# Leaving out the products with a zero state, and padding a triangular tile to 65 columns

## The chip, the cores and the metric

The kernel runs on one core of a Trainium2 chip. A core has five engines with a queue each: TensorE (PE, matrix products), VectorE (DVE), ScalarE (ACT), GpSimd (POOL), and SyncE (SP), which here only issues DMAs. The metric is the device time of one execution in microseconds (us); lower is better. The median of three runs of the kernel before is 2276.57 us (2274.77 to 2276.88).

## The reference

A trunk of two layers over 1024 positions and 1024 channels. A layer normalizes `x`, modulates it by a condition vector, projects it to 8320 columns, runs three causal mixers side by side, gates and merges them, and projects back. Two of the mixers carry a state through the sequence.

```python
# retention, 4 heads of 128, in chunks of C = 128 positions
def step(R, kv_n):
    return chunk_decay * R + kv_n, R
_, R_prev = lax.scan(step, jnp.zeros((B, H, dh, dh)), jnp.moveaxis(kv, 2, 0))
o = o_intra + einsum('bhnid,bhnde->bhnie', q_dec, R_prev)

# RWKV-7, 8 heads of 64, position by position
def step(S, inp):
    r_t, w_t, k_t, v_t, a_t, b_t = inp
    sa = einsum('bhvk,bhk->bhv', S, a_t)
    S = S * w_t[:, :, None, :] + sa[..., None] * b_t[:, :, None, :] + v_t[..., None] * k_t[:, :, None, :]
    return S, einsum('bhvk,bhk->bhv', S, r_t)
_, y = lax.scan(step, jnp.zeros((B, H, N, N)), xs)
```

Both states start at zero, and neither is returned.

## The kernel before

**Large products.** Almost all of PE's time goes to projections. Operands are split into a high and a low part of a faster 32-bit type, and each product is done as three: high by high, high by low, low by high, with 128x128 weights and 512 columns each. These are the groups `acc<-hhi,wh` and their like. Weights come by DMA as `wr`, ACT rounds them into `wh`, and POOL subtracts to get `wl`; `wh` and `wl` have three buffers each. A part of the projection is done late with combined matrices (Strassen's scheme), seen as `acc<-T,wh`.

**Small products.** The mixers use plain 32-bit products (F32), each of which PE does in two passes, so it stands in the trace as two records. A transpose on PE is one record.

**Retention** (`ret_task`): one task per head and layer, eight in all. A task works on two halves `h` of 512 positions, four chunks each: scores `rs`, transposed keys `rkt` (scaled as ACT takes them out), transposed values `rvt`, the chunk products `rkv`, then DVE chains the states `R`, and `ro` adds up the result. The eighth chunk's state is made, but no later chunk reads it.

**RWKV** (`rwkv_task`): one task per pair of heads and layer, eight in all, with 16 chunks of 64 positions each. `prepare` makes the decayed operands `AR` and `BK`; `scores` transposes `BK` into `BKt` (tile `bt`) and makes the triangular matrices `G`: 32 blocks of 128 columns, block `16*hd + c` for head `hd` and chunk `c`. `invert` and `blocks` invert the triangles in place; `states` multiplies `G` by the values into `AV` (tile `av`). After that the 16 chunks are stepped through, each as:

- ACT: `SP` is the state `S` times the chunk's decay `pc`.
- PE: `cy = AR^T S` (`two<-S,AR`), in one half of a PSUM tile `two`.
- DVE: `xst` is `cy` rows 64 to 127 plus `AV`.
- PE: `ch = G^T xst`, one product per head (`ch<-xst,G`); ACT copies it into `Z`.
- PE: `BKt^T Z` into `ch` (`ch<-Z,BKt`); DVE: the new state `S` from it and `SP`, one instruction per head.
- PE: `G^T Z` added to `cy` (`two<-Z,G`); ACT copies that to the output `y`.

In `av` and `ch` the weights are `G`'s columns from 64 of a block on, 65 of them, so that one column belongs to the next block and its result row is not used. The last block has no next one, and there 64 columns are taken (`n = min(65, ...)`).

**Order.** The generators only describe work. `Log.plan` takes all instructions with their dependences and modelled durations and builds one order for every engine: at each point the engine that is free first takes the ready instruction with the smallest key, and RWKV's work has a head start in it (`BIAS`). Every engine then runs its own list in that order. A tile comes from a pool with a fixed number of buffers, and the first instruction that touches a tile waits until a buffer is free. `G` has one buffer, which the RWKV tasks take in turn and which other stages of the layer use too (`gtile`).

Of the kernel before, what the change touches and what calls it, by code (L numbers as in the profile page):

```python
# [9 lines left out]
F32 = mybir.dt.float32  # L10
# [3 lines left out]
ALU = mybir.AluOpType  # L14
# [3 lines left out]
P = 128  # L18
# [538 lines left out]
def trunk_kernel(ctx, tc, xT, cvec, pos, vecs, consts, w_ada, w_all, pool_w, lora_w, out):  # L557
    nc = Log(tc.nc, tc)

    def pool(name, bufs, **kw):  # L560
        return PoolProxy(nc, ctx.enter_context(tc.tile_pool(name=name, bufs=bufs, **kw)), bufs, "")
# [1 line left out]
    cp = pool("cp", 1)  # L563
    hp_ = pool("hb", 32)
    wp = pool("wp", 2)
    gp = pool("gp", 1)
    rp = pool("rp", 4)
    tp = pool("tp", 4)
    mp = pool("mp", 4)
    sb = pool("sb", 1)  # L570
    sp = pool("sp", 2)
# [5 lines left out]
    uid = [0]  # L577

    def gtile(s):
        return gp.tile([P, 32 * P], F32, tag="G", name=nm(s))  # L580

    pin = lambda o: o

    def nm(s):
        uid[0] += 1
        return f"{s}_{uid[0]}"
# [624 lines left out]
    def ret_task(l, hd, qT, kT, vT, sg):  # L1211
        gC = math.exp(math.log1p(-(2.0 ** (-5.0 - hd))) * 128)
        dm = cs("causal", P).unsqueeze(1).to_broadcast([P, 4, P])
        hc = lambda k: cst[:, CST[k] + hd : CST[k] + hd + 1]
        tl, rg, eps_rh = hc("tail"), hc("rowg"), hc("reps")
        v3 = lambda t: t.rearrange("p (c n) -> p c n", n=P)
        prev = None
        for h in range(2):
            cl = lambda t, c: t[:, c * P : (c + 1) * P]
            yield wait(kT[h], qT[h])  # L1220
            ps = mx("rs")
            with nc.together():
                for c in range(4):
                    mmul(cl(ps, c), lhsT=cl(kT[h], c), rhs=cl(qT[h], c), start=True, stop=True)
            sm = mo("rsm")
            nc.vector.scalar_tensor_tensor(v3(sm), v3(ps), rg, dm, op0=ALU.mult, op1=ALU.mult)
            yield 1300
            yield wait(kT[h])
            ps = mx("rkt")
            with nc.together():  # L1230
                for c in range(4):
                    trans(cl(ps, c), cl(kT[h], c))
            kt = mo("rkt")
            nc.scalar.activation(kt, ps, AF.Copy, scale=tl)
            yield 900
            yield wait(vT[h])
            ps = mx("rvt")
            with nc.together():
                for c in range(4):
                    trans(cl(ps, c), cl(vT[h], c))  # L1240
            vt = mo("rvt")
            nc.scalar.copy(vt, ps)
            yield 600
            yield wait(kt, vt, spare=1000)
            kv = mx("rkv")
            with nc.together():
                for c in range(4):
                    mmul(cl(kv, c), lhsT=cl(kt, c), rhs=cl(vt, c), start=True, stop=True)
            R = []
            for c in range(4):  # L1250
                R.append(prev)
                nx = sb.tile([P, P], F32, tag="R", name=nm("R"), bufs=4)
                if prev is None:
                    nc.vector.tensor_copy(nx, cl(kv, c))
                else:
                    nc.vector.scalar_tensor_tensor(nx, prev, gC, cl(kv, c), op0=ALU.mult, op1=ALU.add)
                prev = nx
            yield 600
# [29 lines left out]
    def rwkv_task(l, hp, kT, rT, vp, lt, lw):  # L1288
# [1 line left out]
        AR = r8("AR").rearrange("p (c j t) -> p c j t", j=2, t=CH)  # L1290
        BK = r8("BK").rearrange("p (c j t) -> p c j t", j=2, t=CH)
        Gf = gtile("G")
        G = Gf.rearrange("p (u n) -> p u n", n=P)
        qa = lambda b: slice(64 + 32 * b, 96 + 32 * b)
        BKt = r8("BKt").rearrange("p (c n) -> p c n", n=P)
        Z = r8("Z").rearrange("p (c n) -> p c n", n=P)
# [96 lines left out]
        def scores(h):  # L1393
            yield max(until(whole[h] + 1000), wait(Z, spare=600))
            for q in range(2):
                ps = mx("bt")
                c0 = 8 * h + 4 * q
                with nc.together():
                    for c in range(4):
                        trans(ps[:, c * P : (c + 1) * P], jt(BK, slice(0, P), c0 + c), timed=True)  # L1400
                nc.scalar.copy(BKt[:, c0 : c0 + 4, :], ps.rearrange("p (c n) -> p c n", n=P))
                yield 1300
            for q in range(2):
                c0 = 8 * h + 4 * q
                gps = [mx("g"), cyt()]
                with nc.together():
                    for j in range(4):
                        for hd in range(2):
                            rows = slice(64 * hd, 64 * hd + 64)
                            mmul(gps[hd][:, j * P : (j + 1) * P], jt(BK, rows, c0 + j), jt(AR, rows, c0 + j), timed=True)  # L1410
                for hd in range(2):
                    u0 = 16 * hd + c0
                    nc.vector.tensor_tensor(
                        G[:, u0 : u0 + 4, :], gps[hd].rearrange("p (u n) -> p u n", n=P), rm, op=ALU.mult
                    )
                yield 2600
            yield from bonus(h)
# [46 lines left out]
        def states():  # L1464
            for q in range(4):
                yield wait(G, Z)
                ps = mx("av")
                with nc.together():
                    for j in range(8):
                        c, hd = 4 * q + j // 2, j % 2  # L1470
                        u0 = (16 * hd + c) * P + 64
                        n = min(65, 32 * P - u0)
                        mmul(ps[0:n, j * 64 : j * 64 + 64], Gf[:, u0 : u0 + n], Z[:, c, 64 * hd : 64 * hd + 64])
                nc.scalar.copy(AV[:, q * HF : (q + 1) * HF], ps[0:64, :])
                yield 1500
# [41 lines left out]
        for c in range(16):  # L1517
# [2 lines left out]
            if c % 8 == 0:  # L1520
                y = t_ri("y")
            S, Sn = SS[par], SS[1 - par]
            pcc = pc[:, c : c + 1]
            SP = sb.tile([P, P], F32, tag="SP", name=nm("SP"), bufs=1)
            nc.scalar.activation(SP, S, AF.Copy, scale=pcc)
            cy = cyt()
            sa = mmul(cy[:, 0:P], jt(AR, slice(0, P), c), S)
            if c:
                sa.no_dep = yout[-1]
                sa.after[yout[-1]] = 2  # L1530
            if c > 1:
                sa.own_dep = yout[-2]
            nc.vector.tensor_tensor(xst[0:64, :], cy[64:128, 0:P], AV[:, c * P : (c + 1) * P], op=ALU.add)
            yield wait(xst)
            ch = ps_c.tile([P, HF], F32, tag="ch", name=nm("ch"))
            for hd in range(2):
                cols = slice(64 * hd, 64 * hd + 64)
                u0 = (16 * hd + c) * P
                n = min(65, 32 * P - u0 - 64)
                mmul(ch[0:n, cols], Gf[:, u0 + 64 : u0 + 64 + n], xst[:, cols])  # L1540
            nc.scalar.copy(Z[0:64, c, :], ch[0:64, 0:P])
            yield wait(Z)
            mmul(ch[:, P : 2 * P], BKt[:, c, :], Z[:, c, :])
            for hd in range(2):
                rw = slice(64 * hd, 64 * hd + 64)
                nc.vector.scalar_tensor_tensor(
                    Sn[rw, rw], ch[rw, P + 64 * hd : P + 64 * hd + 64], pc[rw, c : c + 1], SP[rw, rw],
                    op0=ALU.mult, op1=ALU.add,
                )
# [854 lines left out]
```

## Time and profile before

| | |
|---|---|
| median of three runs | 2276.57 us (2274.77 to 2276.88) |
| span of the profiled execution | 2272.5 us; no other time is given for that execution, and the median stands 4.07 us above its span |
| PE busy | 2243.5 us, 99% |
| DVE, ACT, POOL busy | 71%, 41%, 28% |
| granted PE clock over the span | 0.996 |

How to read the profile's rows: a row of a group names the engine, the operation, the tile written and the tiles read, the shape, the number of records, busy time and the mean duration of one. Products overlap in PE's pipeline, so the mean of one (390 to 402 ns for a large product) is longer than the step from one start to the next. What a product costs PE is read from the timeline, whose rows begin with start and duration in us: the start of the next row minus the start of this one. Rows with "x4" merge neighbouring records of one kind. Idle time stands in brackets with what ended it.

### The profile page before, as it was taken

To read this page: it belongs to the slowest core of one execution; us is meant where nothing else is said; L and a number is where in the kernel's file an instruction comes from. 1 tells how busy PE (TensorE), PEld (TensorE's weight loads), DVE (VectorE), ACT (ScalarE), POOL (GpSimd) and SP (SyncE) were. 2 spreads that over 40 slices of the span, in tenths; PEclk is the share of its full clock that TensorE was granted. 3 is DMA by queue.
4 is the path that set the end of the run, shared out by engine and by line. 5 is a ranking of instruction groups with operands and counts; after the bars stand their busy time and mean duration, and the time that the engine had idled before them with its cause. 6 is when DMAs were issued, how large, how long until landed. Compare 5 with 4: busy or idle time off the path is not lost.

```text
span 2272.5 us, 35073 instructions
## 1 busy us (share of the span) xinstructions
PE 2243.5 (99%) x13076; PEld 1865.8 (82%) x13076; DVE 1612.3 (71%) x2776; ACT 934.5 (41%) x1795; POOL 629.1 (28%) x552
## 2 busy tenths in 40 slices
PE   7999999999999999999999999999999999999998
PEld 6788888888888888888888888888888888888888
DVE  7997786867878765677677678687785744465854
ACT  5644434434244334323454444344433444441243
POOL 2223323322326221331232232333431500041211
PEclk9999999999999999999999999999999999999999
DMA  9212111112236563654531111111112533256442
GB/s 323 70 56 68 33 47 39 52 43 62 89 112 228 195 216 112 228 191 165 174 129 38 38 38 35 56 43 48 53 62 84 190 117 112 88 181 217 134 130 84
DMA packets 138042, 248.85 MB, mean 110 GB/s; under 512 B 15632, under 2 KB 18960, under 8 KB 137872
## 3 DMA queue, kind: packets, MB, share of 16 engines
q1 hardware_dynamic: 137872, 246.61, 33.2%
q8 instruction: 103, 1.69, 0.3%
q14 instruction: 67, 0.55, 0.1%
HBM read 187.04 MB, written 59.51 MB: 108 GB/s over the span
## 4 chain that ended last, share of the span: by engine, by line
PE 90%; DVE 7%; ACT 1%; issue 1%; DMA 0%; POOL 0%; DVEq 0%; ACTq 0%; POOLq 0%
PE acc L543 74%; PE two L543 3%; PE ch L543 2%; PE g L543 1%; PE av L543 1%; PE ro L543 1%; DVE ksq L543 1%; PE m L543 1%; PE bt L543 1%; PE lw L543 1%; PE rkv L543 1%; PE rs L543 1%; DVE ada_ps L543 0%; DVE G L543 0%; PE pps L543 0%
## 5 line engine op out<-in xcount | busy, mean ns | idle before, releaser
L543 PE MATMUL acc<-hhi,wh 128*128 128x512 f32 x1488 | 597.9, 402 | 0.0
L543 PE MATMUL acc<-hhi,wl 128*128 128x512 f32 x1488 | 596.9, 401 | 0.0
L543 PE MATMUL acc<-hlo,wh 128*128 128x512 f32 x1488 | 596.2, 401 | 0.0
L543 POOL TENSOR_TENSOR wl<-wr,wh 128x512 fp32r<-128x512 f32 x167 | 225.4, 1351 | 568.0 <-ACT wh L543 421.8
L543 PEld LDWEIGHTS acc<-hhi,wh 128*128 128x128 f32 x1488 | 280.6, 189 | 49.8 <-issue 1.8
L543 PEld LDWEIGHTS acc<-hlo,wh 128*128 128x128 f32 x1488 | 280.5, 189 | 49.3 <-issue 1.1
L543 PEld LDWEIGHTS acc<-hhi,wl 128*128 128x128 f32 x1488 | 280.4, 188 | 49.4 <-issue 0.7
L543 ACT CAST wh<-wr 128x512 fp32r<-128x512 f32 x242 | 149.3, 617 | 265.7 <-PE acc L543 204.7
L543 PE MATMUL acc<-T,wh 128*128 128x512 f32 x576 | 178.2, 390 | 0.0
L543 DVE SCALAR_TENSOR_TENSOR S<-ch,pc,SP 64x64 f32<-64x64 f32 x256 | 72.2, 282 | 87.1 <-PE ch L543 84.0
L543 PEld LDWEIGHTS acc<-T,wh 128*128 128x128 f32 x576 | 108.0, 188 | 22.4
L543 PE MATMUL acc<-T,wl 128*128 128x512 f32 x288 | 112.4, 390 | 0.0
L543 DVE TENSOR_TENSOR wl<-wsum,wh 128x512 fp32r<-128x512 f32 x69 | 49.2, 712 | 81.8 <-ACT wh L543 81.5
L543 ACT CAST wh<-wsum 128x512 fp32r<-128x512 f32 x96 | 59.5, 620 | 95.0 <-PE acc L543 92.9
L543 POOL TENSOR_TENSOR oz<-ol,oz 128x512 fp32r<-128x512 f32 x10 | 14.0, 1401 | 281.7 <-DVE wl L543 212.6
L543 DVE TENSOR_TENSOR xst<-two,MT 64x128 f32<-64x128 f32 x128 | 37.6, 293 | 68.4 <-PE two L543 47.7
L543 DVE TENSOR_TENSOR two<-two,tm 64x30 f32<-64x30 f32 (+14 forms) x240 | 78.9, 329 | 7.3
L543 ACT COPY Z<-ch 64x128 f32<-64x128 f32 x128 | 33.0, 258 | 123.3 <-PE ch L543 123.2
L543 DVE TENSOR_TENSOR tm<-MT,two 64x30 f32<-64x30 f32 (+14 forms) x240 | 76.3, 318 | 10.2 <-ACT two L543 3.4
L543 PE MATMUL acc<-oy,wh 128*128 128x512 f32 x256 | 80.1, 394 | 0.0
L543 PE MATMUL acc<-oz,wh 128*128 128x512 f32 x256 | 79.0, 389 | 0.0
L543 PE MATMUL acc<-oG,wh 128*128 128x512 f32 x256 | 78.9, 389 | 0.0
(329 smaller groups left out, 4890.3 us busy)
## 6 DMA issues: line engine op xcount, KB each, us to landing
wr<-in_w_all SPq DMA_DIRECT2D x268, 256.0 KB, 2.6
wraw<-in_w_all SPq DMA_DIRECT2D x96, 256.0 KB, 2.8
gd<-gsg SPq DMA_DIRECT2D x96, 256.0 KB, 2.0
gs<-gd SPq DMA_DIRECT2D x96, 256.0 KB, 3.5
wada<-in_w_ada SPq DMA_DIRECT2D x80, 256.0 KB, 3.4
ol<-od SPq DMA_DIRECT2D x48, 256.0 KB, 3.3
traw<-hd SPq DMA_DIRECT2D x32, 256.0 KB, 3.1
x<-in_xT SPq DMA_DIRECT2D x16, 256.0 KB, 4.9
```

What stands on the lines that cost most here:

```text
L543: o.inst = f(*a, **k)
```

## The change

- `rwkv_task`, chunk 0: `AR^T S` is left out, as is `SP`. `xst` is copied from `AV` by ACT. The new state is `ch` times the decay, and `two<-Z,G` begins its sum instead of adding to one.
- `rwkv_task`, chunk 15: `SP`, `BKt^T Z` and the two instructions of the new state are left out, and with them the 16th transpose in `scores`.
- `ret_task`, second half: three chunks instead of four in `rkt`, its copy and `rkv`, and one step fewer of `R`.
- `G` is 16 columns wider; POOL sets column 4096 to zero at the start of each task, and the last block takes 65 columns as the others do.
- The pool of `G` is laid out behind two others.

```diff
-    gp = pool("gp", 1)
     rp = pool("rp", 4)
     tp = pool("tp", 4)
+    gp = pool("gp", 1)
...
-        return gp.tile([P, 32 * P], F32, tag="G", name=nm(s))
+        return gp.tile([P, 32 * P + 16], F32, tag="G", name=nm(s))
...
+            nkv = 4 - h
             with nc.together():
-                for c in range(4):
+                for c in range(nkv):
                     trans(cl(ps, c), cl(kT[h], c))
-            kt = mo("rkt")
-            nc.scalar.activation(kt, ps, AF.Copy, scale=tl)
+            kt = mo("rkt")[:, 0 : nkv * P]
+            nc.scalar.activation(kt, ps[:, 0 : nkv * P], AF.Copy, scale=tl)
...
-                for c in range(4):
+                for c in range(nkv):
                     mmul(cl(kv, c), lhsT=cl(kt, c), rhs=cl(vt, c), start=True, stop=True)
             R = []
             for c in range(4):
                 R.append(prev)
+                if c == nkv:
+                    break
...
-        G = Gf.rearrange("p (u n) -> p u n", n=P)
+        G = Gf[:, 0 : 32 * P].rearrange("p (u n) -> p u n", n=P)
+        nc.gpsimd.memset(Gf[:, 32 * P : 32 * P + 1], 0.0)
...
+                n = min(4, 15 - c0)
                 with nc.together():
-                    for c in range(4):
+                    for c in range(n):
                         trans(ps[:, c * P : (c + 1) * P], jt(BK, slice(0, P), c0 + c), timed=True)
...
-                        n = min(65, 32 * P - u0)
+                        n = 65
                         mmul(ps[0:n, j * 64 : j * 64 + 64], Gf[:, u0 : u0 + n], Z[:, c, 64 * hd : 64 * hd + 64])
...
-            SP = sb.tile([P, P], F32, tag="SP", name=nm("SP"), bufs=1)
-            nc.scalar.activation(SP, S, AF.Copy, scale=pcc)
             cy = cyt()
-            sa = mmul(cy[:, 0:P], jt(AR, slice(0, P), c), S)
-            if c:
+            if c == 0:
+                nc.scalar.copy(xst[0:64, :], AV[:, 0:P])
+            else:
+                if c < 15:
+                    SP = sb.tile([P, P], F32, tag="SP", name=nm("SP"), bufs=1)
+                    nc.scalar.activation(SP, S, AF.Copy, scale=pc[:, c : c + 1])
+                sa = mmul(cy[:, 0:P], jt(AR, slice(0, P), c), S)
...
-                n = min(65, 32 * P - u0 - 64)
+                n = 65
                 mmul(ch[0:n, cols], Gf[:, u0 + 64 : u0 + 64 + n], xst[:, cols])
...
-            mmul(ch[:, P : 2 * P], BKt[:, c, :], Z[:, c, :])
-            for hd in range(2):
+            if c < 15:
+                mmul(ch[:, P : 2 * P], BKt[:, c, :], Z[:, c, :])
+            for hd in range(2 if c < 15 else 0):
...
+                if c == 0:
+                    nc.vector.tensor_scalar_mul(Sn[rw, rw], new, pc[rw, 0:1])
...
-                    start=False,
+                    start=c == 0,
```

More of the change, by code (lines that the diff above doesn't have):

```diff
@@ L1397, in scores @@
                 c0 = 8 * h + 4 * q
+                n = min(4, 15 - c0)
                 with nc.together():
-                    for c in range(4):
+                    for c in range(n):
                         trans(ps[:, c * P : (c + 1) * P], jt(BK, slice(0, P), c0 + c), timed=True)
-                nc.scalar.copy(BKt[:, c0 : c0 + 4, :], ps.rearrange("p (c n) -> p c n", n=P))
+                nc.scalar.copy(BKt[:, c0 : c0 + n, :], ps[:, 0 : n * P].rearrange("p (c n) -> p c n", n=P))
                 yield 1300
@@ L1522, in rwkv_task @@
             S, Sn = SS[par], SS[1 - par]
-            pcc = pc[:, c : c + 1]
-            SP = sb.tile([P, P], F32, tag="SP", name=nm("SP"), bufs=1)
-            nc.scalar.activation(SP, S, AF.Copy, scale=pcc)
             cy = cyt()
-            sa = mmul(cy[:, 0:P], jt(AR, slice(0, P), c), S)
-            if c:
+            if c == 0:
[5 more added lines that the diff above has]
+                sa = mmul(cy[:, 0:P], jt(AR, slice(0, P), c), S)
                 sa.no_dep = yout[-1]
                 sa.after[yout[-1]] = 2
-            if c > 1:
-                sa.own_dep = yout[-2]
-            nc.vector.tensor_tensor(xst[0:64, :], cy[64:128, 0:P], AV[:, c * P : (c + 1) * P], op=ALU.add)
+                if c > 1:
+                    sa.own_dep = yout[-2]
+                nc.vector.tensor_tensor(xst[0:64, :], cy[64:128, 0:P], AV[:, c * P : (c + 1) * P], op=ALU.add)
             yield wait(xst)
@@ L1542, in rwkv_task @@
             yield wait(Z)
-            mmul(ch[:, P : 2 * P], BKt[:, c, :], Z[:, c, :])
-            for hd in range(2):
+            if c < 15:
+                mmul(ch[:, P : 2 * P], BKt[:, c, :], Z[:, c, :])
+            for hd in range(2 if c < 15 else 0):
                 rw = slice(64 * hd, 64 * hd + 64)
[L1546 to L1549, printed above, removed]
+                new = ch[rw, P + 64 * hd : P + 64 * hd + 64]
+                if c == 0:
+                    nc.vector.tensor_scalar_mul(Sn[rw, rw], new, pc[rw, 0:1])
+                else:
+                    nc.vector.scalar_tensor_tensor(
+                        Sn[rw, rw], new, pc[rw, c : c + 1], SP[rw, rw], op0=ALU.mult, op1=ALU.add
+                    )
             yield 500
```

## The prediction

> **What bounds the kernel now.** I read the page first, for the share of each engine and the chain that ended last, and then its groups.
>
> ```profile
> span 2272.5 us, 35073 instructions
> ...
> PE 2243.5 (99%) x13076; PEld 1865.8 (82%) x13076; DVE 1612.3 (71%) x2776; ACT 934.5 (41%) x1795; POOL 629.1 (28%) x552
> ...
> PE 90%; DVE 7%; ACT 1%; issue 1%; DMA 0%; POOL 0%; DVEq 0%; ACTq 0%; POOLq 0%
> ...
> L543 PE MATMUL acc<-hhi,wh 128*128 128x512 f32 x1488 | 597.9, 402 | 0.0
> L543 PE MATMUL acc<-T,wh 128*128 128x512 f32 x576 | 178.2, 390 | 0.0
> ```
>
> PE is busy for 99% of the span and carries 90% of the chain that ended last. The two group rows are the same product in two surroundings: 390 ns where large products follow each other (`T`), 402 ns where the mixers' small ones lie between them (`hhi`). I come back to those 12 ns.
>
> A share over the whole span can hide a stage in which PE waits, so I looked at stretches: one in which the first layer's RWKV and retention run, and one of large products alone.
>
> ```profile
> core 0: us, PE busy (x) PEld busy (x) DVE busy (x) ACT busy (x) POOL busy (x), PEclk, DMA share, GB/s
> 85.00:170.00 85.00, 84.60 (x594) 68.93 (x593) 79.11 (x145) 38.37 (x66) 21.98 (x24) 1.00 0.15 44
> 1806.00:2209.00 403.00, 403.00 (x1775) 332.85 (x1775) 233.74 (x303) 155.52 (x269) 71.51 (x50) 1.00 0.44 147
> ```
>
> In the mixers' stretch PE idles 0.40 us of 85, at full clock. DVE has 79 of 85, close behind. So the mixers' long dependent chains do not set the time: the written order fills their gaps with large products. A product taken out of PE's list lets everything behind it move up by what it cost there. In the second stretch 1775 products take 403 us, 0.227 us each: that is the step of a large product that nothing disturbs, and 0.23 below.
>
> **What each removed product costs.** Not the mean duration counts, but the step from its start to the next start. PE's timeline from the last blocks of the inverse to chunk 1 of the last RWKV task gives most prices:
>
> ```profile
> 1692.07 0.19 PE L543 MATMUL two<-G,MT 32*32 32x32 f32 x1
> 1692.19 0.50 PE L543 MATMUL acc<-hhi,wh 128*128 128x512 f32 x1
> 1692.53 0.40 PE L543 MATMUL acc<-hlo,wh 128*128 128x512 f32 x1
> ...
> 1694.67 0.49 PE L543 MATMUL two<-S,AR 128*128 128x128 f32 x2
> 1694.92 0.47 PE L543 MATMUL acc<-hhi,wl 128*128 128x512 f32 x1
> 1695.23 0.39 PE L543 MATMUL acc<-hhi,wh 128*128 128x512 f32 x1
> ...
> 1697.42 0.38 PE L543 MATMUL ch<-Z,BKt 128*128 128x128 f32 x2
> 1697.64 0.40 PE L543 MATMUL two<-Z,G 128*65 128x64 f32 x4
> ...
> 1700.51 0.40 PE L543 MATMUL ch<-xst,G 128*65 128x64 f32 x4
> 1700.72 0.47 PE L543 MATMUL acc<-hhi,wh 128*128 128x512 f32 x1
> ```
>
> - `two<-S,AR` of chunk 0 (row 1694.67): 0.25 us to the next start, and the large product after it takes 0.31 (1694.92 to 1695.23) instead of 0.23. Without it that product stands right behind the 32x32 blocks, as at 1692.19, where it takes 0.34. So 0.25 - 0.03 = 0.22 us goes. Eight tasks: 1.76 us.
> - `ch<-Z,BKt` of chunk 15: 0.22 us from its start to that of `two<-Z,G` (row 1697.42, the same product in chunk 0). What follows it stays, so nothing is lost at the edges. Eight tasks: 1.76 us. It is two passes of 128 columns, hence 0.11 us a pass.
> - the 16th transpose `bt` and the eighth `rkt`: one pass of 128 columns each, 0.11 us. Eight tasks of both: 0.88 + 0.88 us.
> - the eighth `rkv`: two such passes, 0.22 us. Eight tasks: 1.76 us.
>
> **The padding.** A row of the group view and the timeline of chunk 15 in the last task show what the 64-column products cost; the third fence is the stretch around the third and fourth group of `av` in another task.
>
> ```profile
> L543 PE MATMUL bt<-cst,BK 128*128 128x128 f32 x128 | 17.6, 273 | 0.5 <-DVE R L543 0.5
> ...
> L543 PE MATMUL av<-Z,G 128*64 128x64 f32 x16 | 2.6, 246 | 0.0
> L543 PE MATMUL ch<-xst,G 128*64 128x64 f32 x16 | 2.6, 246 | 0.0
> ```
>
> ```profile
> 1754.10 0.54 PE L543 MATMUL ch<-xst,G 128*65 128x64 f32 x4
> ...
> 1754.57 0.66 PE L543 MATMUL rkt<-cst,rk 128*128 128x128 f32 x4
> ```
>
> ```profile
> 1228.78 0.70 PE L543 MATMUL av<-Z,G 128*65 128x64 f32 x9
> 1229.29 0.48 PE L543 MATMUL acc<-hhi,wh 128*128 128x512 f32 x1
> 1229.60 3.14 PE L543 MATMUL av<-Z,G 128*65 128x64 f32 x48
> 1232.67 0.50 PE L543 MATMUL acc<-hlo,wh 128*128 128x512 f32 x1
> 1233.01 0.39 PE L543 MATMUL acc<-hhi,wl 128*128 128x512 f32 x1
> ```
>
> Sixteen records of each are eight products: one `av` and one `ch` per task. The mean of 246 ns says little; the step does. In chunk 15 the four records of `ch`, two of them 64 wide, hold PE for 0.47 us (1754.10 to 1754.57); the same four, all 65 wide, hold it for 0.21 (1700.51 to 1700.72). That is 0.26 us more. The large product after a 64-wide one then takes 0.34 (1232.67 to 1233.01), after a 65-wide one 0.31 (1229.29 to 1229.60): 0.03 more. In `av`, nine 65-wide records take 0.51, 0.057 each; 48 at that step would take 2.72, and the run that ends 64 wide takes 3.07: 0.35 more, an upper end, since the nine end with a shorter step. I take 0.26 + 0.03 = 0.29 at 16 places: 4.64 us, and 0.35 + 0.03 = 0.38, or 6.08 us, as the upper end of this term.
>
> The Trainium skill, "TensorEngine Tiling (Array Packing)", section "Key Properties", says that a change of tiling mode drains TensorE; the trace agrees, 0.47 against 0.21 us. Its section "When to Use Tiling" speaks the other way: a stationary side of at most 64 columns is a case for column tiling, up to twice as fast, and by that padding would win nothing; the sum by it would be 7.0 us instead of 11.7. The rows decide for the first.
>
> **What is added, and what hides.** Per task ACT gains one copy of 64x128 and loses two of `SP` and a quarter of two others; DVE loses the addition at chunk 0, two updates at chunk 15 and one `R`. Neither bounds: PE's idle time in the mixers' stretch above is 0.40 us. At chunk 0 `ch` no longer waits for PE, then DVE; it waits for the last copy into `G`, which it needed before as well. I cost all of this at nothing; that cover is PE's list of large products.
>
> POOL gets one memset of a column of `G` per task. It must wait until the previous task has left `G`, and what is queued behind it on POOL is late by that wait: the weights' `wl` above all, for which PE waits next.
>
> ```profile
> L543 POOL MEMSET k<- 128x1 f32 x8 | 1.0, 130 | 0.0
> ```
>
> ```profile
> 236.71 0.21 POOL L543 MEMSET S<- 128x128 f32 x1 [1.70 <-DVE S L543]
> ```
>
> ```profile
> 244.70 0.69 DVE L543 TENSOR_TENSOR G<-g,cst 128x512 f32<-128x512 f32 x1 [1.11 <-PE two L543]
> ```
>
> ```profile
> POOL Z L543 <- PE two L543: 36.2, 5, 11.8
> ```
>
> A memset of one column takes 0.13 us. At the end of the first task POOL is idle and already waits for that end (236.71, for the last state), and `G` is first written by the next task at 244.70. So the memset has 8 us of room before anything needs it. Price: 0 taken, 8 x 0.13 = 1.0 us at the upper end, if each delayed PE by its length. The wider tile and the moved pool change addresses only; no row here gives that a price, and with the same instructions and shapes I take 0.
>
> **Sum.** 1.76 + 1.76 + 0.88 + 0.88 + 1.76 + 4.64 = 11.68 us, of the profiled span 2272.5. The median of the runs lies 4.07 us above that span; I keep this distance, so 2276.57 - 11.7 = 2264.9, rounded to 2265.0.
>
> **What the order may add.** The order is planned anew from other work, so that the mixers' products fall at other places among the large ones. What is at stake can be read off the 12 ns: 402 - 390 ns, over three groups of 1488 (`hhi,wh` and the two beside it, of the same count), is 54 us that switching and short waits cost in the mixers' stages. A tenth more or less of that is 5.4 us, either way. Hence 2259.6 to 2270.4 for this case.
>
> **The rivals.** A change under 0.2%, 4.6 us, can't be told from none here.
>
> 1. *The padding wins nothing*, because it is not the 64 columns but the end of the run that costs. Against it: `av` at 1228.78 ends in a run too, and its step is short. Then 11.68 - 4.64 = 7.04, so 2269.5.
> 2. *The gain is taken up by waits.* DVE has 7% of the chain and 79.11 of 85 us in the mixers' stretch; if PE comes early and stands before a DVE result each time, what left PE's list comes back as idle time. Against it: 0.40 us of idle time in that stretch, before which no such wait is due. All lost: 2276.6; half lost: 2270.7.
> 3. *POOL is held by the new memset*, the case that ends slower. `Z`'s memset shows how POOL can be held for the previous task: 36.2 us in five waits, at most 11.8. If the memset of `G` stands as early in POOL's list, no `wl` is made meanwhile. One split weight serves 24 large products (four blocks, three products, two halves), 24 x 0.227 = 5.4 us; a wait above that starves PE. Six tasks take `G` from a predecessor in their layer, so at 11.8 us each PE loses 6 x 6.4 = 38 us, and the time is 2276.6 - 11.7 + 38 = 2303. Slower than now from (11.7 + 4.6) / 6 = 2.7 us lost each, a wait of 8.1 us. Against it: the order puts an instruction where its inputs are modelled ready, and POOL's wait at 236.71 is 1.70 us.
>
> The Trainium skill, "TensorE: Matmul & The Clock Gate", section "Architectural detail: the array is 16× 32×32, not 1× 128×128", says that GpSimd works its queue strictly in order; that is what rival 3 lives on, and the wait of 11.8 us agrees.
>
> **Chances.** The sum with the order's 5.4 us: 0.71. Better than that, below 2259.6: 0.07. Rival 1: 0.05. Rival 2: 0.13, half of it as no change and half as a smaller gain. Rival 3: 0.04. Within 0.2% is above 2272.0 and below 2281.1: rival 2's 0.06 and 0.04 of a bad order, 0.10. Faster: 0.86; slower: 0.04. The range reaches from 2259.0 to 2272.0: it holds the first case, rival 1 and half of rival 2, and leaves out some 0.17.
>
> **What would show it.** The group rows would have 240 records of `two<-S,AR` and `ch<-Z,BKt`, 120 of `bt`, 112 of `rkv`, 56 of `rkt`, and no `128*64` row of `av` or `ch`. Chunk 15's `ch` would step in 0.21 us, not 0.47, and PE's first chunk would go from the blocks to a large product in 0.12. Rival 1: the step stays at 0.47. Rival 2: idle time of PE in the mixers' stretches grows by some us. Rival 3: a `G` row on POOL with waits of over 5 us. The prediction is wrong if the three large groups' mean moves from 402 ns by more than 1.2 ns (a tenth of 12).

## The result, and the profile after

The changed kernel takes 2269.82 us (median of nine runs, 2267.98 to 2274.26); the kernel before took 2276.39 in the same comparison (nine runs, 2274.77 to 2277.01). The ratio is 0.9974 with a 95% interval of 0.9965 to 0.9983: 6.6 us or 0.26% faster. The forecast was 11.7 us. The profiled execution of the changed kernel took 2269.18 us, 1.8 more than its span.

First the page of the changed kernel: the span and the busy time of each engine.

```profile
span 2267.4 us, 34859 instructions
...
PE 2233.6 (99%) x13012; PEld 1855.6 (82%) x13012; DVE 1597.7 (70%) x2757; ACT 930.4 (41%) x1787; POOL 610.9 (27%) x547
```

PE's busy time fell by 9.9 us (2243.5 to 2233.6), the span by only 5.1. So PE now idles 33.8 us where it idled 29.0. Half of what was taken out of PE's list came back as idle time; the question is where.

The groups by shape say that the change does what it says. Columns: line, engine, operation, tile written and tiles read, shape, records, busy time and mean ns of one, idle time before.

```profile
L543 PE MATMUL ch<-xst,G 128*65 128x64 f32 x512 | 53.3, 224 | 0.8 <-DVE xst L543 0.8
...
L543 PE MATMUL two<-S,AR 128*128 128x128 f32 x240 | 46.6, 275 | 0.2
...
L543 PE MATMUL av<-Z,G 128*65 128x64 f32 x512 | 33.3, 223 | 0.9 <-DVE G L543 0.8
```

The counts are the forecast ones (240 records of `two<-S,AR` and, in rows not shown, 240 of `ch<-Z,BKt`, 120 of `bt`, 112 of `rkv`, 56 of `rkt`), and all 512 records of `av` and of `ch` are 65 wide. One sign came otherwise than forecast: in seven of the eight tasks PE goes from the blocks of the inverse not to a large product but straight to `ch` of the first head, in 0.12 us. In PE's timeline of chunk 15 in the last task, `ch` steps in 0.21 us (1742.99 to 1743.20) instead of 0.47:

```profile
1742.99 0.40 PE L543 MATMUL ch<-xst,G 128*65 128x64 f32 x4
1743.20 0.48 PE L543 MATMUL acc<-hlo,wh 128*128 128x512 f32 x1
```

**Where the time went.** The number of large products (`acc`) that PE has begun by a given moment shows it, because at each moment chosen here both kernels are in a run of large products, 0.227 us each. The rows are stretches of `acc` alone from the start of the span: the stretch, its length, PE's busy time with the count in brackets, clock, DMA share, GB/s. First before, then after.

```profile
0.00:88.00 88.00, 45.26 (x149) 0.94 0.70 247
0.00:694.00 694.00, 515.10 (x1914) 0.99 0.26 86
0.00:709.00 709.00, 530.10 (x1981) 0.99 0.27 89
0.00:1134.00 1134.00, 947.78 (x3800) 1.00 0.38 125
0.00:2000.00 2000.00, 1682.87 (x6703) 1.00 0.32 104
```

```profile
0.00:88.00 88.00, 44.61 (x146) 0.94 0.71 247
0.00:694.00 694.00, 522.89 (x1931) 0.99 0.27 87
0.00:709.00 709.00, 534.50 (x1976) 0.99 0.28 91
0.00:1134.00 1134.00, 951.99 (x3796) 1.00 0.39 125
0.00:2000.00 2000.00, 1689.27 (x6724) 1.00 0.33 104
```

At 88 us, before the first mixer, the changed kernel was 3 products late; up to there PE's list is the same as before. At 694 us, the end of the first layer's mixers, it is 17 ahead: 20 products or 4.5 us won. At 709 us it is 5 behind: 22 products or 5.0 us lost in 15 us. From 1134 us, when the first layer is done, to 2000 us, behind the second layer's mixers, it wins 25 products, 5.7 us, which is nearly half of the forecast 11.68. So the second layer pays what was forecast, the first layer's mixers three quarters of it, and a stretch of 15 us behind them takes back nearly all that the first layer had won.

That stretch is the passage from the mixers to the combined products (`acc<-T,wh`). The timeline of the changed kernel there, all engines, the brackets giving idle time and what ended it:

```profile
691.15 0.92 SPq L543 DMA_DIRECT2D wraw<-in_w_all  x2
...
694.18 0.39 PE L543 MATMUL acc<-hhi,wl 128*128 128x512 f32 x1
...
695.81 0.50 PE L543 MATMUL acc<-hhi,wh 128*128 128x512 f32 x1 [1.25 <-ACT wh L543]
...
696.55 0.73 PE L543 MATMUL acc<-T,wh 128*128 128x512 f32 x2
...
698.17 0.62 ACT L543 CAST wh<-wsum 128x512 fp32r<-128x512 f32 x1 [1.68 <-DVE wsum L543]
...
698.84 0.73 PE L543 MATMUL acc<-T,wh 128*128 128x512 f32 x2 [1.56 <-ACT wh L543]
...
707.55 0.74 PE L543 MATMUL acc<-T,wh 128*128 128x512 f32 x2 [0.58 <-ACT s L543]
```

PE waits 1.25 us before one large product and 1.56 a few products later; a third wait, at 707.55, adds 0.58 us. Each has slower steps around it too: the 45 products from 694.18 to 709.06 take 14.9 us, where 45 x 0.227 = 10.2 would do, so 4.7 us are lost here. The clock is full throughout (1.00 from 694 to 709 us). The weights come late: `wh` waits for the sum `wsum` on DVE, which needs raw weights (`wraw`) that SP asks for only at 691.15. Nothing in the forecast looked at this place.

### The profile page after: what moved, and what is told of

Read it like the earlier page. It is cut to its first block, busy times and chain, and to the rows that moved or that the text cites. A ratio compares the mean times of both kernels' runs of the same rounds, so it can differ in the third digit from the quotient of the medians.

```text
span 2267.4 us, 34859 instructions
## 1 busy us (share of the span) xinstructions
PE 2233.6 (99%) x13012; PEld 1855.6 (82%) x13012; DVE 1597.7 (70%) x2757; ACT 930.4 (41%) x1787; POOL 610.9 (27%) x547
## 4 chain that ended last, share of the span: by engine, by line
PE 90%; DVE 6%; ACT 1%; issue 1%; DMA 1%; SPq 0%; POOL 0%; DVEq 0%; ACTq 0%; POOLq 0%
PE acc L543 75%; PE two L543 3%; PE ch L543 2%; PE av L543 1%; PE g L543 1%; PE ro L543 1%; DVE two L543 1%; DVE tm L543 1%; PE m L543 1%; DVE G L543 1%; PE lw L543 1%; PE bt L543 1%; PE rkv L543 1%; PE pps L543 1%; DMA x<-in_xT 0%
## 5 line engine op out<-in xcount | busy, mean ns | idle before, releaser
L543 DVE SCALAR_TENSOR_TENSOR S<-ch,pc,SP 64x64 f32<-64x64 f32 x224 | 63.0, 281 | 93.0 <-PE ch L543 90.8
L543 DVE TENSOR_TENSOR wl<-wraw,wh 128x512 fp32r<-128x512 f32 x52 | 35.9, 689 | 59.5 <-ACT wh L543 59.3
```

What stands on the lines that cost most here:

```text
L543: o.inst = f(*a, **k)
```

## The experiments

Two kinds of kernel were built. Names that begin with `k_` keep the planned order of the kernel before on every engine: the plan is made for the full work, and only when an instruction is issued is it dropped or replaced. So PE's list in such a kernel is that of before less what is dropped, and two timelines can be laid side by side, product by product. The others are planned anew, as the changed kernel is. Common to the first kind:

```diff
-            for f, a, k, _ in o.calls:
+            for i, (f, a, k, _) in enumerate(o.calls):
+                if i in o.drop:
+                    continue
+                if i in o.swap:
+                    f, a, k = o.swap[i]
```

All twelve results stand in one table. "Gain" is worked out from counts as above: 0.227 us times the products by which a kernel is further than the one before, first layer (1134 us less 88 us) and second layer (2000 us less 1134 us). The ratio and the shift in the median are against runs of the kernel before on the same chip.

| kernel | count at 88, 1134, 2000 us | gain layer 1 | gain layer 2 | both | median us | shift | ratio (95%) |
|---|---|---|---|---|---|---|---|
| before | 149, 3800, 6703 | | | | 2276.39 | | |
| after | 146, 3796, 6724 | -0.2 | 5.7 | 5.4 | 2269.82 | -6.6 | 0.9974 (0.9965 to 0.9983) |
| `k_all` | 139, 3818, 6744 | 6.4 | 5.2 | 11.6 | 2263.66 | -12.5 | 0.9946 (0.9933 to 0.9958) |
| `k_zero` | 136, 3807, 6727 | 4.5 | 3.9 | 8.4 | 2267.73 | -8.4 | 0.9964 (0.9952 to 0.9977) |
| `k_pad` | 143, 3803, 6709 | 2.0 | 0.7 | 2.7 | 2272.36 | -3.8 | 0.9984 (0.9975 to 0.9992) |
| `k_c0` | 139, 3799, 6711 | 2.0 | 2.0 | 4.1 | 2272.07 | -3.2 | 0.9984 (0.9975 to 0.9992) |
| `k_ret` | 148, 3804, 6708 | 1.1 | 0.2 | 1.4 | 2274.74 | -0.5 | 0.9997 (0.9989 to 1.0006) |
| `k_av64` | 148, 3796, 6695 | -0.7 | -0.9 | -1.6 | 2276.70 | +0.6 | 1.0004 (0.9995 to 1.0013) |
| `r_zero` | 146, 3814, 6725 | 3.9 | 1.8 | 5.7 | 2268.97 | -6.5 | 0.9968 (0.9956 to 0.9980) |
| `r_pad` | 143, 3791, 6700 | -0.7 | 1.4 | 0.7 | 2274.98 | -0.5 | 0.9995 (0.9986 to 1.0004) |
| `b_shake1` | 146, 3810, 6699 | 3.0 | -3.2 | -0.2 | 2276.63 | +1.1 | 1.0006 (0.9997 to 1.0014) |
| `a_shake1` | 141, 3792, 6706 | 0.0 | 2.5 | 2.5 | 2272.24 | -3.3 | 0.9986 (0.9977 to 0.9995) |
| `a_seam` | 145, 3776, 6703 | -4.5 | 5.4 | 0.9 | 2274.42 | -0.8 | 0.9996 (0.9987 to 1.0005) |
| `a_load` | 139, 3782, 6715 | -1.8 | 6.8 | 5.0 | 2270.20 | -5.2 | 0.9980 (0.9971 to 0.9989) |

The gain of both layers and the shift of the median agree to about 1 us in every row. That is what makes the split by layers worth reading, though it comes from one execution each. How far one execution can be trusted is seen in the second layer, where the changed kernel, `a_seam` and `a_load` run one order and gain 5.7, 5.4 and 6.8 us: a difference of about 1 us between two rows means little.

### The removals alone, in the old order

`k_all` is the whole change in the order of the kernel before; the copy of `xst` in chunk 0 stays on DVE, where the addition was, and the memset stands ahead of the first write of `G`.

```diff
+            if h:
+                nc.ops[-1].drop = (3,)
...
+            if c in (0, 15):
+                so.drop = (0,)
...
+            if c == 0:
+                sa.drop = (0,)
+                xo.swap[0] = (nc.nc.vector.tensor_copy, (xst[0:64, :], AV[:, 0:P]), {})
...
+            if c == 15:
+                bo.drop = (0,)
```

> The order planned for the kernel before is kept on every engine; from it only the products with the zero state and for the unused last states are left out (with the copies and updates that served them), and the last triangular block is 65 wide, with one memset of G per task on POOL. The xst of chunk 0 is copied by VectorE, where its addition stood. Theory A (prices right, the new order lost the rest): minus 11.7 us, 2264.7, at least 10 us below before. Theory B (the prices were too high, PE waits elsewhere for what it gains): minus 6 to 7 us as in the changed kernel, about 2270.

Measured: 2263.66 us, 12.5 us faster, and 11.6 us by the counts, where the forecast's sum was 11.68. It beats both kernels: the interval of its ratio, 0.9933 to 0.9958, lies below the changed kernel's, 0.9965 to 0.9983. Its page, and its counts around the passage:

```profile
span 2262.8 us, 34896 instructions
...
PE 2234.1 (99%) x13012; PEld 1859.7 (82%) x13012; DVE 1602.6 (71%) x2752; ACT 927.9 (41%) x1779; POOL 628.4 (28%) x560
```

```profile
0.00:694.00 694.00, 519.57 (x1932) 1.00 0.28 88
0.00:709.00 709.00, 534.57 (x1997) 1.00 0.28 90
```

PE is as busy as in the changed kernel (2234.1 and 2233.6 us, 13012 records each), yet it idles 28.7 us, like the kernel before. Between 694 and 709 us it begins 65 products, the kernel before 67, the changed kernel 45. The work is that of the changed kernel; what differs is the order, where eight copies and eight memsets are done, and 13 instructions that the new plan has on DVE instead of POOL.

`k_zero` is `k_all` without the padding, and `k_pad` only the padding, both in the old order:

```diff
+                        if n == 64:
+                            av.swap[j] = (
+                                nc.nc.tensor.matmul, (ps[0:65, j * 64 : j * 64 + 64],),
+                                dict(lhsT=Gf[:, u0 : u0 + 65], rhs=Z[:, c, 64 * hd : 64 * hd + 64], start=True, stop=True),
+                            )
...
+                if n == 64:
+                    cm.swap[0] = (
+                        nc.nc.tensor.matmul, (ch[0:65, cols],),
+                        dict(lhsT=Gf[:, u0 + 64 : u0 + 129], rhs=xst[:, cols], start=True, stop=True),
+                    )
```

> Order of before kept; only the products with the zero state and for the unused states are left out, the 64-wide products stay. Theory A: minus 7.0 us. Theory B: less than 4 us.

> Order of before kept; only the padding: the last block of av and ch is 65 wide, G one column wider with its memset. Theory A: 16 places at 0.29 us, minus 4.6 us. Theory B: less than 3 us. Rival 1 of the prediction (padding wins nothing): 0.

Measured: 8.4 us by both measures for the removed products (forecast 7.04), 2.7 by the counts and 3.8 by the medians for the padding (forecast 4.64). They add up: 8.4 + 2.7 = 11.1 against 11.6 for both together. At its 16 places the padding does shorten PE's steps by the forecast amount, 4.5 us in all (`av` by 0.28 us and `ch` by 0.28 us a task); the rest came back in waits elsewhere.

### The order

`r_zero` is the changed kernel without the 65th column, `r_pad` the kernel before with it; both are planned anew.

```diff
-        nc.gpsimd.memset(Gf[:, 32 * P : 32 * P + 1], 0.0)
...
-                        n = 65
+                        n = min(65, 32 * P - u0)
```

> Changed kernel without the 65th column: the last block takes 64 columns as before and G's extra column is neither set nor read; the order is planned for these instructions. With before's order kept, the same removal gave 8.4 us. Theory A (a new order costs or gives some us, by chance): anywhere within 5 us of that, 2263 to 2273, and another loss than the changed kernel's. Theory B (the removal itself makes the following stages late, whatever the order): about 5 to 6 us less than the kept order, as in the changed kernel, 2273.

> Before with the padding alone, the order planned for it (the memset of G and 65 columns change the modelled work). With before's order kept it gave 3.75 us. Theory A: within 5 us of that, 2267 to 2277. Theory B: no loss against the kept order, since nothing is removed, 2272.

Measured: 6.5 and 0.5 us. The padding is worth 3.8 us in the old order, 0.5 in a new one of its own, and none beside the other removals (`r_zero` takes 2268.97 us, the changed kernel 2269.82). The first layer shows the scatter: `r_zero` wins 3.9 us there; the changed kernel, from which the padding takes some more, loses 0.2.

`b_shake1` and `a_shake1` are the kernel before and the changed one with the keys in the plan of all instructions but RWKV's and the first stage's moved by up to 20 places either way at random.

```diff
-SEED = 0
-SHAKE = 0
+SEED = 1
+SHAKE = 40
```

> Before, with the same work and the planner's keys of all but RWKV's and the first stage's instructions shifted by up to 20 places either way: another order of the same work. Theory A: a shift of some us either way, 2 to 6. Theory B: within 1 us of before.

> The changed kernel with the same shift of keys: another order of the changed work. Theory A: the time scatters by some us around 2267, within 2262 to 2274. Theory B: it stays at 2270, within 1 us.

Measured: the kernel before in another order has the same time within its interval, but only because 3.0 us won in the first layer meet 3.2 lost in the second. The changed kernel in another order loses 3.2 us of its 5.7 in the second layer and so comes out at half its gain. One other order of each is no distribution; it does show that a layer moves by some 3 us when nothing but the order changes.

### The passage at 694 us

`a_seam` takes the changed kernel's order and puts five instructions earlier, to bring the weights sooner: two sums `wsum` on DVE, two casts `wh` on ACT and one `wl` on POOL.

```diff
+        for here, moved in ((4795, (4686, 4689)), (4796, (4717, 4718, 4687))):
+            for i in moved:
+                o = at[i]
+                order.remove(o)
+                order.insert(order.index(at[here]), o)
```

> The changed kernel in its own order, but for five instructions at the end of layer 0's mixers, at 684 to 698 us of its profile: two wsum on VectorE, two wh on ScalarE and one wl on GpSimd stand a few places earlier in their queues, ahead of the T forms and of the copy of acc. PE's order is unchanged. Theory A (the stalls of 1.4, 1.7 and 0.7 us that PE has there come from this order alone): at least two of them go, minus 2 to 3.9 us, 2266 to 2268. Theory B (the weights land late, whatever the order): no change, 2270.

Measured: slower than the changed kernel by some 5 us (2274.42). By the counts 4.3 us of that are in the first layer (-4.5 against -0.2), and 15 products or 3.4 us of them are lost between 694 and 709 us. The timeline of this kernel, and a stretch of it with the clock (the last three numbers: clock, DMA share, GB/s):

```profile
690.12 1.28 SPq L550 DMA_DIRECT2D od<-rob  x1
691.46 0.93 SPq L550 DMA_DIRECT2D wraw<-in_w_all  x2
...
694.26 0.69 DVE L550 TENSOR_TENSOR wsum<-wraw,wraw 128x512 f32<-128x512 f32 x1 [2.36 <-DMA wraw<-in_w_all]
...
700.96 0.80 PE L550 MATMUL acc<-hhi,wh 128*128 128x512 f32 x1 [6.17 <-ACT acc L550]
```

```profile
697.60:704.40 6.80, 3.44 (x8) 0.50 0.60 186
```

Put ahead, `wsum` makes DVE wait 2.36 us for the raw weights, with everything queued behind it; PE pays 6.17 us in one wait. It pays once more behind it: the granted clock is 0.50 from 697.6 to 704.4 us, and the eight large products from 700.96 to 704.49 take 3.5 us instead of 1.8. So the loads are what is late. They come after the store of retention's last result (`od<-rob`) in SP's queue. Either that store holds them there, or they wait for the buffer that `rob` still needs.

`a_load` tells these apart: the two loads stand ahead of two stores on SP (`gd<-gsg`, `od<-rob`), and a cast `wh` ahead of the copy of `acc` on ACT.

```diff
+        for here, moved in ((4536, (4682, 4683)), (4713, (4717,))):
```

> The changed kernel in its own order, but for two places at the end of layer 0's mixers: the third and fourth load of the first combined weights (wraw, issued at 691.15 and about 691.6 us in its profile) stand ahead of the two stores gd<-gsg and od<-rob in SyncE's queue, and ScalarE's wh<-wraw stands ahead of its copy of acc. Everything else, PE's order too, is unchanged. Theory A (the loads are late because SyncE's queue holds them behind stores that wait): they issue by 690 us, the stall of 1.4 us goes and that of 1.7 shrinks, minus 1.4 to 3 us, about 2267 to 2268. Theory B (they wait for their buffers, which retention's last instructions give free, whatever stands before them): they issue at 690 to 691 as before, and the time stays within 1 us of 2270.

Measured: 2270.20 us, the changed kernel's time within the intervals; the first layer is 1.6 us worse, the second 1.1 better in the profiled execution, though there its order is the same. Its timeline, and again a stretch with the clock:

```profile
690.54 0.75 DVE L550 SCALAR_TENSOR_TENSOR rob<-rot,vec,silu 128x512 f32<-128x512 f32 x1 [1.20 <-PE rot L550]
...
691.32 1.53 SPq L550 DMA_DIRECT2D wraw<-in_w_all  x2
...
697.17 0.50 PE L550 MATMUL acc<-hhi,wh 128*128 128x512 f32 x1 [1.19 <-ACT acc L550]
...
700.84 0.50 PE L550 MATMUL acc<-hhi,wl 128*128 128x512 f32 x1 [1.88 <-POOL wl L550]
```

```profile
702.10:705.50 3.40, 3.40 (x10) 0.51 1.00 349
```

First in the queue, the loads still leave only when `rob` is made (690.54 + 0.75 = 691.29; the trace names `rob` as what ended their wait): they wait for a buffer. This execution is 7 products or 1.6 us behind the changed kernel's from its lead-in on, so at 691.32 they leave 1.4 us sooner in the order of the work. The store's 1.2 us come on top in the changed kernel, but without it PE only waits elsewhere, first for a copy of `acc`, then for `wl` on POOL.

Behind these two waits the clock halves here too: a large product steps in 0.43 us, and the nine from 702.10 to 705.75 take 3.65 us where 2.04 would do. These 1.6 us are as much as the first layer lost. In the changed kernel the waits of 1.25 and 1.56 us left the clock at 1.00. So the move of the loads by itself won and cost about nothing up to here; no run shows it at full clock.

In the kernel before, the store of that `rob` leaves SP ten microseconds sooner, and the first combined product comes 1.5 us later. From its timeline, and then from that of the changed kernel:

```profile
679.92 0.32 SPq L543 DMA_DIRECT2D od<-rob  x1
...
698.09 0.62 PE L543 MATMUL acc<-T,wh 128*128 128x512 f32 x2
```

```profile
689.89 1.21 SPq L543 DMA_DIRECT2D od<-rob  x1
```

So the new order does retention's end later and the combined products sooner (696.55), and the weights between have little room. Shown: it is the order, it is this place, and small moves in the queues there cost 1.6 us (`a_load`) to 4.3 us (`a_seam`), of which 1.6 and 1.7 us are the halved clock behind longer waits. Not settled: why the plan puts them so. Its durations are a model; no run here tells a wrong duration from chance.

### The terms

`k_c0` leaves out chunk 0's `SP` and `two<-S,AR`, as in `k_all` (with the copy of `xst`, and the new state and `two<-Z,G` without the left-out terms), and nothing else.

```diff
+            if c == 0:
+                so.drop = (0,)
...
+            if c == 0:
+                sa.drop = (0,)
+                xo.swap[0] = (nc.nc.vector.tensor_copy, (xst[0:64, :], AV[:, 0:P]), {})
```

> Order of before kept, nothing else changed; only chunk 0's product with the zero state goes, with its SP, and xst is copied by VectorE instead of added to. By the price of the prediction: 8 x 0.22 = 1.76 us. If, beside the price, the wait of ch on that product and on the addition was on PE's path, as the kept order with all products removed makes likely (8.4 instead of 7.0): 2.5 to 3.2 us.

Measured: 4.1 us by the counts, 3.2 by the medians, at a price of 1.76. The timeline of the last task says where the rest is; first before, then `k_c0`:

```profile
1695.20 0.58 ACT L543 COPY G<-two 32x512 f32<-32x512 f32 x1 [1.20 <-PE two L543]
...
1695.69 0.40 PE L543 MATMUL acc<-hhi,wl 128*128 128x512 f32 x1
...
1695.81 0.29 DVE L543 TENSOR_TENSOR xst<-two,MT 64x128 f32<-64x128 f32 x1 [1.09 <-ACT G L543]
...
1696.16 0.45 PE L543 MATMUL ch<-xst,G 128*65 128x64 f32 x4
```

```profile
1693.62 0.57 ACT L550 COPY G<-two 32x512 f32<-32x512 f32 x1 [0.78 <-PE two L550]
...
1694.32 0.39 PE L550 MATMUL acc<-hhi,wl 128*128 128x512 f32 x1
1694.56 0.40 PE L550 MATMUL ch<-xst,G 128*65 128x64 f32 x4
```

Before, the large product ahead of `ch` takes 0.47 us to the next start, now 0.24. The removed product stood at the head of a chain: ACT's last copy into `G` began only when that product had ended (at 1695.16), DVE's addition waited for the copy, and PE stood before `ch` until the addition was done (1696.10). In `k_c0` the copy begins at the end of the blocks (1693.58), and `xst` needs no addition behind it. Product, copy and addition follow each other so in all eight tasks of before. The step ahead of `ch` shrinks by 0.23 to 0.26 us in six of them, 1.45 us in all, and the step of `ch` itself from 0.26 to 0.21 us in the same six, 0.3 us in all. The removed product is worth 0.22 us in every task, as forecast; 1.76 + 1.45 + 0.3 make 3.5. The other 0.6 us of the counts lie outside chunk 0.

`k_ret` leaves out the eighth `rkt` (with its part of the copy), `rkv` and one `R`, and nothing else: behind the transposes, behind the chunk products and at the last step of `R` stand

```diff
+            if h:
+                nc.ops[-1].drop = (3,)
...
+                if c == nkv:
+                    nc.ops[-1].drop = (0,)
```

> Order of before kept, nothing else changed; only retention's unused last chunk goes: the eighth rkt, rkv and the last R. By the price of the prediction 0.88 + 1.76 = 2.64 us; if new waits of PE take a part back, 1.5 to 2.2 us.

Measured: 1.4 us by the counts and 0.5 by the medians (the interval of the ratio holds no change), at a price of 2.64. The waits (engine, tile, what it waited for: total us, times, longest), before and then `k_ret`:

```profile
PEld ro L543 <- DVE R L543: 2.3, 8, 0.4
...
PEld rvt L543 <- ACT rkt L543: 0.5, 2, 0.3
```

```profile
PEld ro L550 <- DVE R L550: 2.8, 8, 0.6
...
PEld rvt L550 <- ACT rkt L550: 1.5, 3, 0.6
```

The transposes `rvt` come right behind those of `rkt`. With one `rkt` less, PE reaches them sooner and its weight loads (PEld) stand until ACT has taken `rkt` out: 1.5 us instead of 0.5, and 0.5 us more before `ro`. Side by side with before, the removed products are worth 0.11 and 0.22 us a task, 2.65 us in all, as forecast; but PE's steps grow by 0.8 us ahead of `rvt`, 0.4 ahead of `ro`, 0.3 ahead of one `ch`, and 0.5 at the start of the second layer.

`k_av64` makes all 256 products of `av` 64 wide, in the old order, which leaves their 65th result row unwritten (it is not used).

```diff
+                        av.swap[j] = (
+                            nc.nc.tensor.matmul, (ps[0:64, j * 64 : j * 64 + 64],),
+                            dict(lhsT=Gf[:, u0 : u0 + 64], rhs=Z[:, c, 64 * hd : 64 * hd + 64], start=True, stop=True),
+                        )
```

> Order of before kept and nothing left out; all 256 products of av take 64 columns of G instead of 65 (before: 8 of them). If only the switch into and out of the 64-column shape costs, each of the 32 groups pays it once, 24 groups more than before: plus 24 x 0.29 = 7 us. If each 64-wide pass costs more by itself (0.107 between the two passes of one product in the trace of before, against 0.059 for 65 wide), 248 more products of two passes at 0.048 come on top: plus 24 us more, about 31 us. If 64 columns are as fast as 65: no change.

Measured: +0.6 us, inside its interval, and 1.6 us lost by the counts. Neither +7 us nor +31 us came. The forecast of +7 had the number of visits wrong: in PE's list the 32 groups stand in 16 runs, one of 16 records and one of 48 in each task, and the run of 48 ended 64 wide before. So eight visits to the 64-wide shape are new, not 24, and 8 x 0.29 = 2.3 us were due. PE's timeline of the stretch that the forecast showed for the kernel before:

```profile
1230.65 0.50 PE L550 MATMUL acc<-hhi,wh 128*128 128x512 f32 x1
1231.08 3.01 PE L550 MATMUL av<-Z,G 128*64 128x64 f32 x48
1234.02 0.50 PE L550 MATMUL acc<-hlo,wh 128*128 128x512 f32 x1
1234.35 0.39 PE L550 MATMUL acc<-hhi,wl 128*128 128x512 f32 x1
```

The 48 records step in 2.94 us, 0.061 each, close to the 0.057 of 65-wide ones. From the product ahead to the second behind it takes 0.43 + 2.94 + 0.33 = 3.70 us; before, with only the last of the run 64 wide, 0.31 + 3.07 + 0.34 = 3.72. The eight new visits, at the runs of 16, cost 0.10 to 0.23 us each, 1.1 us in all (PE's steps around both runs of a task, against before). So the cost belongs to the visit, going into the 64-wide shape and out again, not to each product. The Trainium skill, "TensorEngine Tiling (Array Packing)", section "Key Properties", says that a change of tiling mode drains TensorE; this agrees, with 0.061 us inside a run against 0.47 for four records that go in and out.

## Why the prediction was right, and where it was not

The time fell in the range and on the forecast side, 4.8 us above the predicted 2265.0. Point by point:

| term | forecast | steps at its own place, old order | whole kernel in the old order, by counts (shift of the median) |
|---|---|---|---|
| padding, 16 places | 4.64 | 4.5, `k_pad` | 2.7 (3.8), `k_pad` |
| chunk 0, `two<-S,AR` | 1.76 | 1.76, and 1.75 of waits, `k_c0` | 4.1 (3.2), `k_c0` |
| retention, `rkt` and `rkv` | 0.88 + 1.76 | 0.87 + 1.78, `k_ret` | 1.4 (0.5), `k_ret` |
| chunk 15, `ch<-Z,BKt` and `bt` | 1.76 + 0.88 | 1.98 + 0.87, `k_zero` | 2.9: 8.4 - 4.1 - 1.4, not run alone |
| all | 11.68 | 11.8, and 1.75 of waits | 11.6 (12.5), `k_all` |

- **The sum** held in the old order. Its prices held too, each at its own place: PE's steps there shrink by 11.8 us. What was wrong is the nothing that was put beside them. Waits went with chunk 0's product, 1.75 us at the places themselves, and by the counts new ones took back 1.3 us of the retention's price and 1.8 of the padding's. These made up for each other, so that 11.6 meets 11.68 is in part luck.
- **"At chunk 0 `ch` no longer waits for PE, then DVE ... I cost all of this at nothing."** This failed: a wait of some 0.24 us went at six of eight places. The last copy into `G`, which `ch` was to go on waiting for, had itself waited for the removed product. The forecast's own fence of chunk 0 left out the row of `ch` at 1696.16, where it stood.
- **Retention and padding: rival 2 in part.** The local step of the padding came as forecast (0.21 instead of 0.47). But part came back: the wait of `ro`'s weight loads for `R` grew from 2.3 us in 8 times to 3.2 in 11 when nothing but the padding was done:

```profile
PEld ro L550 <- DVE R L550: 3.2, 11, 0.4
```

- Where PE comes early to a short chain through ACT or DVE, it waits. The 0.40 us of idle time in one stretch, on which the forecast rested, says that no wait was long then, not that there is slack for PE to come sooner. Of the retention's price, half or more was lost so.
- **Rival 1** fell: in the old order the padding won 2.7 to 3.8 us. It is not the end of a run that costs, but the change of shape that stood at it, and the padding takes that away. In the new order, though, the padding's gain can't be seen (`r_zero` against the changed kernel).
- **Rival 3** fell. The memset of `G` takes 0.098 us and waits at most 2.4 us:

```profile
L543 POOL MEMSET G<- 128x1 f32 x8 | 0.8, 98 | 13.7 <-PE two L543 11.3 <-issue 1.4 <-DMA xres<-in_xT 0.9
```

- **"What the order may add"**: 5.4 us either way for the whole kernel. By the counts the order cost 11.6 - 5.4 = 6.2 us, by the medians 5.9, just beyond the bound. Its reason failed as well: it was read off the 402 ns of the mixers' large products, durations that overlap, and the mean is still 402 ns in the changed kernel (`acc<-hhi,wh`). The forecast's own test, a mean moved by over 1.2 ns, saw nothing, because most of the loss lies in three waits of PE that start behind the mixers: between 694 and 709 us the changed kernel begins 20 products fewer than `k_all`, 4.5 of the 6.2 us. A mean over a stage can't show a wait at its end.

## What to carry to other kernels

Price a removed product by the step from its start to the next start, and then look at the product that waited on it: the wait goes too, and a neighbour that now comes early may get one. Where a planner builds the order, a small removal buys a new order as well, and that moved a layer here by 3 to 7 us, as much as the removal was worth; keep the old order and drop instructions at issue to measure the removal, and perhaps to ship it (2263.66 against 2269.82 us). To find a loss between two orders, count the steady unit of work begun by fixed moments; here fifteen microseconds out of 2270 held 4.5 of the 6.2 us lost. And a wait can cost twice: two experiments that lengthened PE's waits in one place also halved its clock behind them, for 1.6 and 1.7 us more.

## What was not expected of the hardware

- The lead-in, the first 88 us, has the same instructions in every `k_` kernel as in the kernel before, but by its end PE has begun 136 to 149 large products: up to 13 x 0.227 = 3.0 us between executions. A single span is uncertain by that much, and the counts from 88 us on agree better with the medians. The 14 traces fall into two kinds. In those with 145 to 149 products PE does the 24 products `sums` at 24 to 25 us in 2.7 to 2.8 us, in those with 136 to 143 it takes 5.1; before is of the first kind, `k_c0` of the second:

```profile
24.27 2.74 PE L543 MATMUL sums<-fixed,ringG 128*128 128x1 f32 x24
```

```profile
24.44 5.11 PE L550 MATMUL sums<-fixed,ringG 128*128 128x1 f32 x24
```

- Behind the lead-in executions of one order agree closely, for a while. `a_load` and the changed kernel have one order up to the passage: from 88 to 694 us the one begins 1924 - 139 = 1785 large products, the other 1931 - 146 = 1785. In the second layer, with one order again, they differ by five products, 1.1 us.
- The clock of a kernel that is 99% busy can still halve in its middle: behind waits of 1.19 and 1.88 us within six microseconds (`a_load`) it was 0.51 for 3.4 us, and in and behind a wait of 6.17 us (`a_seam`) 0.50 for 6.8 us. Behind waits of 1.25 and 1.56 us (the changed kernel) it stayed at 1.00. Where the border lies is not shown.
- A 64-wide product costs hardly more in a run of its kind than a 65-wide one (0.061 and 0.057 us a record), but 0.26 us more when it comes alone between full-width products.
